# Inverting a head's diagonal 16-row blocks: substitution in blocks of 4 rows and doubling, in place of fifteen steps

## The chip, the cores and the metric

The kernel runs on one core of one Trainium2 chip. The metric is the device time of one launch in microseconds, the median of several runs. The engines are named as the profile names them: PE (TensorE, matmuls), PEld (its weight loads), DVE (VectorE), ACT (ScalarE), POOL (GpSimd) and SP (SyncE, which issues most of the DMAs). Each engine works through a queue of its own in order, and engines wait for each other by semaphores.

## The reference

One layer of a streaming encoder for 16 meta tokens, 512 tokens of a prompt and 8 x 16 tokens of samples (656 together): layer norm, one input projection, then two groups of heads side by side (a gated delta rule in 8 heads of 128, and a complex diagonal state space of 64 groups), an output projection, layer norm, a gated feed-forward of 2048 by 5632, layer norm. What matters here is the gated delta rule, which is computed block by block; for each block a unit lower triangular system is solved:

```python
a_mat = jnp.where(strict, jnp.einsum('bhnid,bhnjd->bhnij', kb, k) * decay, 0.0)
rhs = jnp.concatenate([v * beta[..., None], kb * jnp.exp(gcum)[..., None]], axis=-1)
sol = lax.linalg.triangular_solve(a_mat, rhs, left_side=True, lower=True, unit_diagonal=True)
w_val, k_cd = sol[..., :dv], sol[..., dv:]
...
def step(s, xs):
    w = w_val_c - jnp.einsum('bhcd,bhde->bhce', k_cd_c, s)
    o = jnp.einsum('bhcd,bhde->bhce', q_dec_c, s) + jnp.einsum('bhij,bhje->bhie', qk_c, w)
    s = s * g_tot_c[..., None, None] + jnp.einsum('bhcd,bhce->bhde', k_dec_c, w)
```

## The kernel before

The stages follow one another: layer norm and the state space's tables, the projections of the state space group, the heads' stage (`heads_phase`, from about 400 to 1000 us), the output projection, and the feed-forward, which is most of the time. In the heads' stage PE's queue is filled with the "fill": the projections q, k, v of heads 2 to 7 and z of all heads (`project`: for each of 16 row tiles and each half of the tokens three matmuls, L505, L506 and L507, on the two parts `whi` and `wlo` of a weight). The weights come in as float32 `raw`; ACT makes `whi` (L160), and in this stage POOL makes `wlo` (L161). The fill's results go through a convolution on DVE (L646, three times L649, L656, L657) and ACT (L634 to L636, L653, L654).

Among the fill's steps `drive` sets side jobs, generators which go on one step at a time; PERIOD = 47 steps of the fill lie between one head and the next. For each head these are

- `delta_prep`: the products k k^T and q k^T of the head's 6 units (tokens in groups of 112, 112, 112, 96, 96 and, for the samples, 128), then `inv16`, then the factors of the units (L839 and others);
- `delta_double`: the inverses grow from 16 rows to a whole unit. POOL makes `gm` (L860), PE multiplies it with `tt` (L863), ACT copies the product (`pp`, L864), PE multiplies again (L868), DVE subtracts it from `rt` (L870); then twice transposes (L393), copies of `tt` on ACT (L877), a product with `gt` (L885, copied by ACT in L886) and one with `rt` (L893);
- `delta_scan`: unit after unit through the state. PE multiplies the state `st` with k and q (L935, L936); DVE makes `rhs` (L938); PE solves with `rt` (L943); ACT scales to `x` (L945); PE makes the output's part (L948) and the state's part (L971); DVE adds the output into `vc` (L953) and updates `st` (L976), for which the next unit's L935 waits. The last unit, that of the samples, has its own path: L923 to L930 on PE, DVE and ACT, then `xm`, x spread over four masks (L958, DVE), and PE's L963 on it; POOL scales the samples' states `sb` (L964) and DVE adds to them (L967).

The scan of one head runs beside the preparation of the next ones. A tile scheduler sets the order of each engine's queue from these jobs, by its own estimates of the time at which an instruction can begin.

`inv16` inverts the 41 diagonal blocks of 16 rows of a head's units. Three DMAs bring `gt` to memory (L752), three fetch the blocks so that each block lies on a partition of its own (`blk`, 41 partitions x 16 x 16, L754). `t0` is set to the identity. Then for each column i from 1 to 15 a multiply of a column of `blk` (step of 16 elements) with the i x i corner of `t0` into `pr` (L760, i x i products) and a reduce of these along their rows (L762); every step needs the one before. A transposed copy (L765) makes the second half of `ti`, and six DMAs to memory (L768) and six back (L771) put both into `tt` and `rt`. The generator yields four times within the fifteen steps. In gelu, which runs in the same stage for the state space group, L1315 is a multiply of 128 x 640 elements, and L1318 one that writes with a step of four elements.

## Time and profile before

| | us |
| --- | --- |
| median of the runs (lowest, highest) | 3027.91 (3024.25, 3028.52) |
| the profiled execution: span | 3024.3 |
| PE busy | 2846.3 (94%) |
| PEld busy | 2721.0 (90%) |
| DVE busy | 2312.0 (76%) |
| ACT busy | 1171.5 (39%) |
| POOL busy | 595.9 (20%) |

The span is that of one execution on the profiler; there is nothing around it that a run's time would add. The chain of work that ended last, followed back from the end, has 53% of the span on PE, 13% on DVE, 3% on DMA and 1% each on ACT and POOL; 1% of the span in this chain is DVE's L760. The heads' stage is 600 us of the 3024.3. In the rows further down the first number is a start in microseconds from the start of the span and the second the duration, both in microseconds; what stands in brackets is the idle time of the engine in front of that row, and what ended it. In the table by stretches the column PEclk is the granted clock of PE as a share of 2.4 GHz (0.5 is 1.2 GHz).

### The profile page before, as it was taken

Reading aid. Unit: us, or ns where it says so; the run is one execution under the profiler, and the core shown is the slowest. Engines: PE = TensorE matmul, PEld = TensorE weight load, DVE = VectorE, ACT = ScalarE, POOL = GpSimd, SP = SyncE. Lnnn points to the kernel's source line nnn. Section 1 sums busy time; section 2 is a strip of 40 time slices with the busy share of each in tenths; the row PEclk is TensorE's granted clock in tenths of the full one; section 3 lists DMA queues with packets and bytes.
Section 4 is the critical chain, followed back from the end, with each engine's and each line's share of the span. In section 5 each row is a group of like instructions: output and inputs, shape, how many; then the busy total and the mean of one; then the engine's idle time right before and its main releaser. Section 6 shows DMA issues by size and latency. Waiting matters only on the chain.

```text
span 3024.3 us, 47836 instructions
## 1 busy us (share of the span) xinstructions
PE 2846.3 (94%) x18707; PEld 2721.0 (90%) x18707; DVE 2312.0 (76%) x4077; ACT 1171.5 (39%) x2127; POOL 595.9 (20%) x551
## 2 busy tenths in 40 slices
PE   5989899999999999979999999999999999999996
PEld 4989888888888978779999999999999999999995
DVE  8899867666665663697777777777777879888998
ACT  4445334333343522553333333333333443332334
POOL 4244423222222040240000000000000023321214
PEclk9999999899899999989999999999999999999998
DMA  4333333333344753543333333333343534433533
GB/s 152 84 103 98 96 105 84 80 82 86 90 134 141 244 167 103 170 121 118 101 115 99 115 103 113 113 113 112 105 119 99 168 115 145 131 115 115 174 120 125
DMA packets 460770, 360.67 MB, mean 119 GB/s; under 512 B 49364, under 2 KB 422276, under 8 KB 456432
## 3 DMA queue, kind: packets, MB, share of 16 engines
q1 hardware_dynamic: 458744, 354.50, 39.3%
q8 instruction: 147, 2.41, 0.3%
q10 hardware_dynamic: 1800, 3.11, 0.3%
q14 instruction: 79, 0.65, 0.1%
HBM read 295.55 MB, written 62.01 MB: 118 GB/s over the span
## 4 chain that ended last, share of the span: by engine, by line
PE 53%; DVE 13%; issue 4%; DMA 3%; ACT 1%; POOL 1%; SPq 0%; DVEq 0%; ACTq 0%; POOLq 0%
PE pb_m L1393 16%; PE pb_m L1392 16%; PE pb_m L1391 16%; DVE wlo L161 3%; DVE acf L1804 2%; DVE raw L193 2%; DMA rq<-in_ffn_w_down 1%; PE pj L505 1%; PE pj L506 1%; ACT whi L160 1%; PE pj L507 1%; POOL wlo L161 1%; DVE acc L1487 1%; DVE hp L1778 1%; DVE pr L760 1%
## 5 line engine op out<-in xcount | busy, mean ns | idle before, releaser
L160 ACT ACTIVATE whi<-raw 128x1024 fp32r<-128x1024 f32 x408 | 431.6, 1058 | 768.0 <-PE pb_m L1392 259.8
L161 DVE TENSOR_TENSOR wlo<-raw,whi 128x1024 fp32r<-128x1024 f32 x330 | 426.4, 1292 | 221.8 <-ACT whi L160 221.4
L505 PE MATMUL pj<-hh,whi 128*128 128x328 f32 (+1 forms) x1248 | 429.4, 344 | 1.9 <-DVE zs L1006 1.2
L506 PE MATMUL pj<-hl,whi 128*128 128x328 f32 (+1 forms) x1248 | 404.4, 324 | 0.0
L507 PE MATMUL pj<-hh,wlo 128*128 128x328 f32 (+1 forms) x1248 | 403.0, 323 | 0.0
L1393 PE MATMUL pb_m<-hp,wlo 128*128 128x320 f32 x1120 | 348.6, 311 | 21.9 <-DVE wlo L161 18.9
L1391 PE MATMUL pb_m<-hp,whi 128*128 128x320 f32 x1120 | 347.4, 310 | 2.2 <-ACT whi L160 2.2
L1392 PE MATMUL pb_m<-hp,whi 128*128 128x320 f32 x1120 | 346.9, 310 | 0.0
L160 ACT ACTIVATE whi<-rq 128x1024 fp32r<-128x1024 f32 x190 | 200.6, 1058 | 324.1 <-PE pb_m L1392 309.2
L161 POOL TENSOR_TENSOR wlo<-raw,whi 128x1024 fp32r<-128x1024 f32 x78 | 197.4, 2531 | 580.9 <-ACT whi L160 487.4
L1778 POOL TENSOR_TENSOR hp<-lq,hp 128x960 fp32r<-128x960 f32 (+1 forms) x16 | 47.5, 2976 | 1106.8 <-ACT hp L1777 1106.8
L505 PEld LDWEIGHTS pj<-hh,whi 128*128 128x128 f32 x1248 | 243.7, 195 | 12.4 <-issue 8.2
L506 PEld LDWEIGHTS pj<-hl,whi 128*128 128x128 f32 x1248 | 244.3, 196 | 2.1 <-issue 1.5
L507 PEld LDWEIGHTS pj<-hh,wlo 128*128 128x128 f32 x1248 | 243.7, 195 | 2.1 <-issue 1.5
L1393 PEld LDWEIGHTS pb_m<-hp,wlo 128*128 128x128 f32 x1120 | 211.7, 189 | 25.6 <-DVE wlo L161 21.7
L193 DVE TENSOR_TENSOR raw<-rq 128x1024 f32<-128x1024 f32 x128 | 163.4, 1276 | 86.9 <-DMA rq<-in_ffn_w_up 34.2
L161 DVE TENSOR_TENSOR wlo<-rq,whi 128x1024 fp32r<-128x1024 f32 x176 | 223.4, 1270 | 4.3 <-ACT whi L160 2.9
L1391 PEld LDWEIGHTS pb_m<-hp,whi 128*128 128x128 f32 x1120 | 211.8, 189 | 3.3 <-ACT whi L160 3.3
L1392 PEld LDWEIGHTS pb_m<-hp,whi 128*128 128x128 f32 x1120 | 211.6, 189 | 0.0
L1708 DVE TENSOR_TENSOR s<-pb_m,s 128x320 f32<-128x320 f32 x308 | 149.2, 485 | 71.9 <-PE pb_m L1393 69.3
L1804 DVE TENSOR_TENSOR acf<-acf,pb_m 128x320 f32<-128x320 f32 x368 | 163.4, 477 | 22.3 <-PE pb_m L1393 20.8
L1391 PE MATMUL pb_m<-T1h,whi 128*128 128x320 f32 x352 | 110.3, 313 | 2.6 <-ACT T1h L1544 2.6
(561 smaller groups left out, 7631.7 us busy)
## 6 DMA issues: line engine op xcount, KB each, us to landing
rq<-in_ffn_w_gate SPq DMA_DIRECT2D x88, 512.0 KB
rq<-in_ffn_w_up SPq DMA_DIRECT2D x88, 512.0 KB
raw<-in_w_in SPq DMA_DIRECT2D x80, 512.0 KB
rq<-in_ffn_w_down SPq DMA_DIRECT2D x80, 512.0 KB
raw<-in_w_out SPq DMA_DIRECT2D x48, 512.0 KB
scr_h<-hq SPq DMA_DIRECT2D x20, 1120.0 KB
lq<-scr_h SPq DMA_DIRECT2D x16, 640.0 KB
raw<-in_ffn_w_down SPq DMA_DIRECT2D x16, 512.0 KB
```

The costliest lines, as they stand in the source:

```text
L160: nc.scalar.activation(hi, val, AF.Copy)
L161: next(self.lows).tensor_sub(lo, val, hi.bitcast(F32))
L193: self.nc.vector.tensor_tensor(o, x, y, op=op)
L505: nc.tensor.matmul(o, whi[:, k], self.h_hi[u][:, k, s], start=(kk == 0), stop=False)
L506: nc.tensor.matmul(o, whi[:, k], self.h_lo[u][:, k, s], start=False, stop=False)
L507: self.last = nc.tensor.matmul(o, wlo[:, k], self.h_hi[u][:, k, s], start=False, stop=(kk == KT - 1))
L1391: mm(out, sh, mh, start=first, stop=False)
L1392: mm(out, sh, ml, start=False, stop=False)
L1393: self.last = mm(out, sl, mh, start=False, stop=last)
L1708: v.tensor_tensor(t, x, y, op=ALU.add)
L1778: (v if (j + g) % 2 else nc.gpsimd).tensor_sub(x[:, 1], t, x[:, 0].bitcast(F32))
L1804: v.tensor_tensor(x, x, ps, op=ALU.subtract if o[0] == "-" else ALU.add)
```

## The change

In place of fifteen steps over columns the block of 16 rows is inverted in three stages. First N is negated in place (L762). Then the four diagonal blocks of 4 rows are inverted at once, by substitution: a copy of 4 elements, and for columns 2 and 3 a multiply (L767, 16 and 36 products) and a reduce (L768). `blk`, `ti` and `pr` are wider (272 and 576 elements), so that the four blocks, which lie 68 elements apart, can be written as one access pattern. Then two doublings, from 4 to 8 and from 8 to 16 rows: each makes the block above the diagonal as T11 N12 T22, in two products. A product is a multiply (L782; for s = 4 twice 64 elements, for s = 8 once 512, patterns of four dimensions with a step of 16 elements in one operand) and reduces (L790 to the middle part of `pr`, L788 into `t0`). The copy and the DMAs behind it are as they were. The generator still yields four times: behind the substitution, behind both products for 4, and behind the first product for 8.

DVE has 20 instructions for a head where it had 33 (two memsets, a copy and thirty others before). Other lines of the diff take comments out, which moves line numbers behind `inv16` by 28: L935, L953, L976 are now L963, L981, L1004; L864, L870, L877 are L892, L898, L905; L958 and L963 (`xm` and its matmul) are L986 and L991.

```diff
-        blk = dl.tile([nb, 16, 16], F32, name="blk", tag="blk", bufs=1)
-        ti = dl.tile([nb, 2, 16, 16], F32, name="ti", tag="ti", bufs=1)
-        pr = dl.tile([nb, 225], F32, name="pr", tag="pr", bufs=1)
+        bk = dl.tile([nb, 272], F32, name="blk", tag="blk", bufs=1)
+        tk = dl.tile([nb, 2, 272], F32, name="ti", tag="ti", bufs=1)
+        pr = dl.tile([nb, 576], F32, name="pr", tag="pr", bufs=1)
+        whole = lambda x: x[:, :256].rearrange("b (c i) -> b c i", i=16)
+        fours = lambda x: x.rearrange("b (n x) -> b n x", x=68)[:, :, :64].rearrange("b n (c i) -> b n c i", i=16)[:, :, :, :4]
+        blk, t0, t1 = whole(bk), whole(tk[:, 0]), whole(tk[:, 1])
...
-        t0 = ti[:, 0]
-        v.memset(t0, 0.0)
-        v.memset(t0.rearrange("b c i -> b (c i)")[:, ::17], 1.0)
-        for i in range(1, 16):
-            p = pr[:, : i * i].rearrange("b (c j) -> b c j", j=i)
-            v.scalar_tensor_tensor(p, blk[:, :i, i][:, None, :].to_broadcast([nb, i, i]), -1.0, t0[:, :i, :i],
-                                   op0=ALU.mult, op1=ALU.mult)
-            v.tensor_reduce(t0[:, :i, i], p, axis=mybir.AxisListType.X, op=ALU.add)
-            if i in (4, 8, 11, 13):
-                yield
-        v.tensor_copy(ti[:, 1].rearrange("b i c -> b c i"), t0)
+        v.memset(tk[:, 0], 0.0)
+        v.memset(tk[:, 0, 0:256:17], 1.0)
+
+        v.tensor_scalar(bk[:, :256], bk[:, :256], -1.0, None, op0=ALU.mult)
+        b4, t4 = fours(bk), fours(tk[:, 0])
+        v.tensor_copy(t4[:, :, 0, 1], b4[:, :, 0, 1])
+        for i in (2, 3):
+            p = pr[:, : 4 * i * i].rearrange("b (n c j) -> b n c j", n=4, j=i)
+            v.tensor_tensor(p, b4[:, :, :i, i][:, :, None, :].to_broadcast([nb, 4, i, i]), t4[:, :, :i, :i], op=ALU.mult)
+            v.tensor_reduce(t4[:, :, :i, i], p, axis=mybir.AxisListType.X, op=ALU.add)
+        yield
+
+        for s in (4, 8):
+            n = 8 // s
+            mid = pr[:, 512 : 512 + n * s * s]
+            for right in range(2):
+                for k in range(n):
+                    lo, hi = slice(2 * s * k, 2 * s * k + s), slice(2 * s * k + s, 2 * s * k + 2 * s)
+                    p = pr[:, k * s**3 : (k + 1) * s**3].rearrange("b (r c k) -> b r c k", c=s, k=s)
+                    if right:
+                        x, y = mid[:, k * s * s : (k + 1) * s * s].rearrange("b (r c) -> b r c", c=s), t0[:, hi, hi]
+                    else:
+                        x, y = t0[:, lo, lo], blk[:, lo, hi]
+                    v.tensor_tensor(p, x[:, :, None, :].to_broadcast([nb, s, s, s]),
+                                    y.rearrange("b k c -> b c k")[:, None].to_broadcast([nb, s, s, s]), op=ALU.mult)
+                if right:
+                    for k in range(n):
+                        lo, hi = slice(2 * s * k, 2 * s * k + s), slice(2 * s * k + s, 2 * s * k + 2 * s)
+                        p = pr[:, k * s**3 : (k + 1) * s**3].rearrange("b (r c k) -> b r c k", c=s, k=s)
+                        v.tensor_reduce(t0[:, lo, hi], p, axis=mybir.AxisListType.X, op=ALU.add)
+                else:
+                    v.tensor_reduce(mid, pr[:, : n * s**3].rearrange("b (x k) -> b x k", k=s), axis=mybir.AxisListType.X, op=ALU.add)
+                if s == 4 or not right:
+                    yield
+        v.tensor_copy(t1.rearrange("b i c -> b c i"), t0)
         for c in range(2):
             for g in range(3):
-                nc.sync.dma_start(self.diag(sr[c], g), ti[rows[g], c])
+                nc.sync.dma_start(self.diag(sr[c], g), (t0, t1)[c][rows[g]])
```

The scheduler gives other orders between about 410 and 950 us; ahead of that and behind it the queues are the same. Three places follow. The first is DVE's queue within `inv16` of head 1, at about 469 us before: L953 and L976 belong to the scan of head 0. Before:

```order
L760 SCALAR_TENSOR_TENSOR pr<-blk,ti 41x49
L953 TENSOR_TENSOR vc<-o_5610,ps_seq 96x128
L762 TENSOR_REDUCE ti<-pr 41x7
L976 SCALAR_TENSOR_TENSOR st<-st,ee,ps_seq 128x128
L760 SCALAR_TENSOR_TENSOR pr<-blk,ti 41x64
```
After:

```order
L782 TENSOR_TENSOR pr<-pr,ti 41x64 x2
L788 TENSOR_REDUCE ti<-pr 41x4x4 x2
L782 TENSOR_TENSOR pr<-ti,blk 41x512
L790 TENSOR_REDUCE pr<-pr 41x64
L981 TENSOR_TENSOR vc<-o_5584,ps_seq 96x128
L782 TENSOR_TENSOR pr<-pr,ti 41x512
L1004 SCALAR_TENSOR_TENSOR st<-st,ee,ps_seq 128x128
L788 TENSOR_REDUCE ti<-pr 41x8x8
```
L953 and L976 (now L981 and L1004) stood between two small pairs; now one stands between the two wide multiplies and the other behind the second.

The second is DVE's queue in the samples' part of head 4's scan, at about 773 us before. Before:

```order
L930 SCALAR_TENSOR_TENSOR o_9003<-ps_seq,own,o_9003 128x128
L646 TENSOR_SCALAR yc<-xp,cwc 128x680
L649 SCALAR_TENSOR_TENSOR yc<-xp,cwc,yc 128x680 x2
L953 TENSOR_TENSOR vc<-o_9003,ps_seq 128x128
L958 TENSOR_TENSOR xm<-x,consts 128x512
L649 SCALAR_TENSOR_TENSOR yc<-xp,cwc,yc 128x680
L967 TENSOR_TENSOR sb<-sb,ps_seq 128x512
```
After:

```order
L958 SCALAR_TENSOR_TENSOR o_8925<-ps_seq,own,o_8925 128x128
L646 TENSOR_SCALAR yc<-xp,cwc 128x680
L649 SCALAR_TENSOR_TENSOR yc<-xp,cwc,yc 128x680 x2
L898 TENSOR_TENSOR rt<-rt,ps_inv 96x5x3x16
L986 TENSOR_TENSOR xm<-x,consts 128x512
L981 TENSOR_TENSOR vc<-o_8925,ps_seq 128x128
L649 SCALAR_TENSOR_TENSOR yc<-xp,cwc,yc 128x680
L995 TENSOR_TENSOR sb<-sb,ps_seq 128x512
```
`xm` still follows two of the three L649, but the doubling's subtraction (L870, now L898), which stood further back, is now in front of it.

The third is ACT's queue at the same place. Before:

```order
L929 ACTIVATE o_9003<-ps_seq,own 128x128
L945 ACTIVATE x<-ps_seq,fc 128x128
L160 ACTIVATE whi<-raw 128x1024
L954 ACTIVATE jk_9075,ms<-vc 128x128
L653 ACTIVATE kq<-yc 128x528
L864 ACTIVATE pp_4510<-ps_inv 96x15x16
L654 ACTIVATE kq<-yc 128x128
L877 ACTIVATE tt<-ps_inv 32x5x32
L877 ACTIVATE tt<-ps_inv 32x3x32
```
After:

```order
L957 ACTIVATE o_8925<-ps_seq,own 128x128
L973 ACTIVATE x<-ps_seq,fc 128x128
L892 ACTIVATE pp_4510<-ps_inv 96x15x16
L905 ACTIVATE tt<-ps_inv 32x5x32
L905 ACTIVATE tt<-ps_inv 32x3x32
L982 ACTIVATE jk_8997,ms<-vc 128x128
L160 ACTIVATE whi<-raw 128x1024
L914 ACTIVATE pp<-ps_inv 32x5x32
```
L160, which makes the next `whi` and which POOL's L161 waits for, stood behind `x` (L945); it now stands behind the doubling's copies L892 and L905 and L982.

## Rows read from the trace of the kernel before

**Rows 1.** The page, busy time of each engine (share of the span), instructions:

```profile
PE 2846.3 (94%) x18707; PEld 2721.0 (90%) x18707; DVE 2312.0 (76%) x4077; ACT 1171.5 (39%) x2127; POOL 595.9 (20%) x551
```

**Rows 2.** Table by stretch: length; busy PE, PEld, DVE, ACT, POOL; PEclk, DMA share, GB/s:

```profile
400.00:1100.00 700.00, 658.45 (x4421) 596.85 (x4420) 474.58 (x1241) 281.08 (x843) 203.18 (x148) 0.94 0.43 121
630.00:646.00 16.00, 14.35 (x69) 9.65 (x68) 8.94 (x30) 2.41 (x9) 0.85 (x2) 0.57 0.30 83
776.00:796.00 20.00, 17.50 (x88) 13.07 (x87) 9.37 (x29) 3.53 (x11) 0.99 (x1) 0.57 0.22 57
919.00:926.00 7.00, 4.97 (x34) 4.38 (x34) 3.56 (x11) 1.45 (x6) 1.90 (x1) 0.76 0.37 74
```

**Rows 3.** Groups of DVE, 400 to 1000 us: count | busy us, mean ns | idle before:

```profile
L760 DVE SCALAR_TENSOR_TENSOR pr<-blk,ti 41x1 f32<-41x1 f32 (+14 forms) x120 | 62.9, 524 | 3.9 <-DMA blk<-scr_g 0.9
...
L762 DVE TENSOR_REDUCE ti<-pr 41x1 f32<-41x1 f32 (+14 forms) x120 | 27.7, 231 | 3.1
```

**Rows 4.** Timeline of DVE in inv16, heads 1 and 7:

```profile
466.36 0.14 DVE L760 SCALAR_TENSOR_TENSOR pr<-blk,ti 41x1 f32<-41x1 f32 x1
...
469.33 0.33 DVE L976 SCALAR_TENSOR_TENSOR st<-st,ee,ps_seq 128x128 f32<-128x128 f32 x1
...
471.36 2.04 DVE L760 SCALAR_TENSOR_TENSOR pr<-blk,ti 41x121 f32<-41x121 f32 x1
...
476.40 0.55 DVE L760 SCALAR_TENSOR_TENSOR pr<-blk,ti 41x225 f32<-41x225 f32 x1
476.99 0.38 DVE L762 TENSOR_REDUCE ti<-pr 41x15 f32<-41x225 f32 x1
...
905.09 0.14 DVE L760 SCALAR_TENSOR_TENSOR pr<-blk,ti 41x1 f32<-41x1 f32 x1
```

**Rows 5.** Timeline of POOL in head 1 and in scans 2 and 4:

```profile
470.76 2.49 POOL L161 TENSOR_TENSOR wlo<-raw,whi 128x1024 fp32r<-128x1024 f32 x1 [7.05 <-ACT whi L160]
...
625.78 2.39 POOL L161 TENSOR_TENSOR wlo<-raw,whi 128x1024 fp32r<-128x1024 f32 x1 [4.41 <-ACT whi L160]
...
773.95 3.05 POOL L161 TENSOR_TENSOR wlo<-raw,whi 128x1024 fp32r<-128x1024 f32 x1 [1.64 <-ACT whi L160]
```

**Rows 6.** Single lines on DVE: duration in ns, min/median/max:

```profile
L958 DVE TENSOR_TENSOR xm<-x,consts x8: 677/678/685, 487.8 to 988.3; 128x512 f32<-128x512 f32 x8
...
L1318 DVE SCALAR_TENSOR_TENSOR ge<-gt__9621,yf x1: 1284/1284/1284, 837.8 to 837.8; 128x640 f32<-128x640 f32 x1
...
L649 DVE SCALAR_TENSOR_TENSOR yc<-xp,cwc,yc x72: 900/919/2911, 146.9 to 810.6; 128x680 f32<-128x680 f32 x72
```

**Rows 7.** Waits of PE from 400 to 1000 us: total us, times, longest:

```profile
PE ps_seq L935 <- DVE st L976: 8.8, 8, 3.0
PE ps_seq L963 <- DVE xm L958: 6.4, 3, 2.5
PE ps_seq L943 <- DVE rhs L938: 3.3, 3, 1.5
...
PE ps_seq L923 <- DVE vc L953: 3.0, 3, 2.0
```

**Rows 8.** Timeline of PE where its waits end:

```profile
470.84 0.38 PE L935 MATMUL ps_seq<-st,kq 128*96 128x128 f32 x2
...
632.02 1.22 PE L963 MATMUL ps_seq<-xm,kd 64*128 64x512 f32 x1 [1.65 <-DVE xm L958]
...
778.57 1.97 PE L963 MATMUL ps_seq<-xm,kd 64*128 64x512 f32 x2 [2.50 <-DVE xm L958]
...
911.43 0.46 PE L935 MATMUL ps_seq<-st,kq 128*96 128x128 f32 x2 [1.65 <-DVE st L976]
...
921.04 1.07 PE L923 MATMUL ps_seq<-sb,kq 128*32 128x256 f32 x16 [2.03 <-DVE vc L953]
```

**Rows 9.** Timeline of DVE ahead of xm in scans 2 and 4:

```profile
625.98 5.38 DVE L649 SCALAR_TENSOR_TENSOR yc<-xp,cwc,yc 128x680 f32<-128x680 f32 x2
...
773.85 3.87 DVE L649 SCALAR_TENSOR_TENSOR yc<-xp,cwc,yc 128x680 f32<-128x680 f32 x2
```

## The prediction

> **What bounds the kernel now.** I read the engines' busy times first: PE is busy for 94% of the span, DVE for 76%, POOL for 20% [rows 1]. So a shorter DVE chain is worth only what PE now waits for it. The change touches the heads' stage alone, and the table by stretches shows there, from 400 to 1100 us, 658.45 of 700 us of PE and a mean clock of 0.94 [rows 2]: some 42 us of idle and, as 0.06 of 700, another 42 us lost to half clock. In the same table three short stretches stand at 0.57, 0.57 and 0.76 [rows 2], each from the end of one wait of PE [rows 8]: the granted clock falls from 2.4 to 1.2 GHz behind such waits, and stays there for longer than the wait was. The third view is the list of PE's waits in this stage [rows 7]: DVE's state update L976 (8.8 us), DVE's `xm` L958 (6.4), `rhs` L938 (3.3), `vc` L953 (3.0). All four are short operations that stand in DVE's queue among the instructions of `inv16` or behind them. The last view is the timeline of DVE in head 1 [rows 4]: fifteen pairs of multiply and reduce, one waiting for the other, from 466.36 to 477.37, 11.0 us, and a copy behind them; four other instructions, which the scan of the head before needs, stand between them.
>
> **The change: DVE's own time.** By the groups of DVE instructions, L760 took 62.9 us in 120 instructions and L762 27.7 [rows 3]. One clean multiply is 0.14 us for one product and 0.55 for 225 [rows 4], so 0.14 + 1.8 ns a product; 1240 products in 15 instructions are 2.1 + 2.23 = 4.33 us a head, 34.7 in eight. The other 28.2 us are stalls: the 121-product multiply took 2.04 us, and POOL's L161 ran from 470.76 to 473.25 beside it [rows 4, 5]. A reduce is 0.38 for 225 [rows 4], so 0.14 + 1.07 ns a product, 27.7 / 8 = 3.46 a head; I see no stalled reduce.
> After: multiplies on 16, 36, four times 64 and twice 512 products, 8 x 0.14 + 1332 x 1.8 ns = 3.52; reduces on 16, 36, 128, 64, 64, 512, 512, 7 x 0.14 + 1332 x 1.07 ns = 2.41; the negation of 256 elements between the smallest multiply and that of 225 products, 0.14 and 0.55 [rows 4], taken at 0.25 because it reads one operand as the reduce does; the copy of four 0.14. Together 6.32 against 7.79, and 13 instructions fewer, each with about 0.04 us to the next (476.95 to 476.99) [rows 4], 0.52: 2.0 us a head, 16 in all. The memsets and the transposed copy stay.
> The wide multiply has no row. A 512-element product with both operands read along rows took 0.68 (L958); one of 640 elements with a step of four elements on its output took 1.28, 2.0 ns an element (L1318) [rows 6]. So one of 512 costs 0.68 to 1.16; I take 0.14 + 0.92 = 1.06, from the line through L760's rows, because its column operand has the same step of 16 elements. Both together move a head by -0.8 to +0.2.
> [...]
> Stalls: 28.2 / 8 = 3.5 us a head, so a chain is 11.0 - 1.7 (head 1's own stall) + 3.5 = 12.8 us on average; one that is two to four us shorter and spends less time in two-operand multiplies (3.5 for 4.3) should keep about 2.6. That is 0.9 a head, 7 in all. DVE's busy time falls by some 23 us (16 without the stalls' part, 30 with the low price of the wide multiply). None of it is time of the span yet: PE has its fill, the projections' matmuls L505 to L507, for nearly all of it.
>
> **What of it reaches PE.** The chain ends about 2 us earlier where no stall falls out and 4 or 5 where one of some 2 us does. The doubling behind it (L863, L868, now L891, L896) moves 2 to 7 triples of the fill forward in PE's queue, and with it everything on ACT and DVE.
> Gains. (a) Waits in which PE stood for something of DVE that was held up by a stalled multiply: L943's 3.3, of which I count two thirds, 2.2, and L923's 3.0, whose `vc` stood behind the end of the chain (the longest, 2.03, at 921.04) [rows 7, 8]: 5.2 us together; and the fall of the clock behind the last, 7 x 0.24 = 1.7 [rows 2]. (b) Scan 4: PE waited 2.50 us for `xm` at 778.57 [rows 8], because two L649 in front of it took 3.87 us in place of 1.84 (0.92 each in the median), stalled by POOL's L161 from 773.95 [rows 5, 6, 9]. That L161 waits for ACT's L160; in the new order L160 stands behind the doubling's copies L892 and L905, so the POOL operation starts behind the two L649. PE has `xm` when it comes for it: 2.50 + (1 - 0.57) x 20 = 11.1 us [rows 2]. (c) Scan 2 likewise: 1.65 at 632.02, two L649 of 5.38 us under L161 from 625.78 [rows 5, 8, 9]; L160 moves behind L905, and PE's order has the doubling's first product and transposes well ahead of `xm`. 1.65 + 0.43 x 16 = 8.5 us [rows 2]. In scans 1 and 3 PE's waits of the same kind keep their neighbours, and I leave them as they are.
> Costs. (d) The new wait. Fifteen small pairs let a scan's L953 and L976 in after at most half a microsecond; the new order puts them behind the wide products. In head 1 L976 ended at 469.66 and PE came for it at 470.84 [rows 4, 8]. Now it (L1004) stands behind the second wide multiply: 6.32 - 0.69 for the last reduce, + 0.3 for L981 + 16 x 0.04 = 6.6 into the chain, end at 466.36 + 6.6 + 0.33 = 473.3, so 2.4 us late; and POOL's L161 from 470.76 [rows 5] then lies on a wide multiply, so up to 2 more: 4.3. In head 7 it stands behind both wide multiplies and two operations of gelu (0.83 and 1.28, as L1318 [rows 6]): 9.0 us into the chain, which began at 905.09, against 6.3 (L935 waited for it until 911.43) [rows 4, 8]: 2.7. In heads 2 to 6 it stands behind the second wide multiply (2), the first (3 to 5) or the copy (6), by the same sum 0.3 to 1.7 us later each, 4.9 together; there is no slack to take it, since L935 waited for L976 8 times [rows 7]. Sum 11.9 us, between 7 (no stall meets a wide multiply, and half of the small ones are hidden) and 16. Queued behind L1004 on DVE are the rest of the chain and the next `rhs`; who waits for it is PE's L935, and in PE's queue the whole fill stands behind that. (e) Waits of two us and more bring the clock down: the one of 2.03 us cost 1.7 [rows 2, 8], the one of 1.65 before 911.43 none that I see. I count three new falls, 5.1 us (none to five).
> DMAs: the number and the order of the transfers of a head are the same (3, 3, 6, 6), nothing passes SP's queue, and `tt` comes earlier with the end of the chain.
> Sum: -5.2 - 1.7 - 11.1 - 8.5 + 11.9 + 5.1 = -9.5 us. The profiled execution's span of 3024.3 us is that of the fastest of the three runs, 3.6 below their median; so 3024.3 - 9.5 + 3.6 = about **3018 us**.
>
> **Rivals.** (B) No change: one of the two `xm` waits stays or a new one of its size comes. `xm` in scan 2 is only about a microsecond earlier by the queue (a POOL product L964 that now comes first would hold L656 instead, and L898 is now in front of `xm`). For it: the new order puts L898 ahead of `xm` in four scans, and L898 waits for PE. Against: PE's own `xm` matmuls stand further back. With one of (b), (c) lost the sum is -1 to +2: 3027 to 3030 us. (C) Slower: the wide multiplies are where stalls now land. Of the 120 multiplies of 0.14 to 0.55 us some 13 were held up (28.2 us by 2.1 each); one of 1.06, with L1004 behind it, is met oftener, and in each such head PE waits 2 us more and loses 1.7 to the clock. If it is so in six heads and not in two, (d) and (e) grow by 4 x 3.7 = 15, and (c) is lost for the same reason: -9.5 + 15 + 8.5 = +14, 3042 us. It decides from the fourth head on in which L1004 ends behind a stalled wide multiply. For it speaks 28.2 us of stalls in this very line; against, that the chain is shorter. (D) The change doesn't do what it says: the wide products, of four dimensions, run at 2.1 us each with nothing beside them, twice my price; then a head's chain is no shorter than before (-2.0 + 2.1), the doubling is no earlier, neither `xm` wait goes (+19.6), and L1004 is another 1 to 2 us later in six heads: about +19, 3047 us.
>
> **How the numbers follow.** Forecast 0.50, B 0.25, C 0.19, D 0.06. About 0.2%, 6 us, is what a measurement of this kernel can tell from no change. The forecast's case holds sums from -20 ((d) at 7, no new falls) to -3, so a tenth of it counts as no change, and a part of B goes beyond 6 us on either side: faster 0.51, same 0.25, slower 0.24. The range goes from the forecast's best sum, 3024.3 - 20 + 3.6 = 3008, less 2 for the low price of the wide multiplies, to most of C: 3006 to 3037 us.
>
> **What would show it.** In the changed kernel's profile: 120 and 120 instructions replaced by 64 multiplies and 56 reduces, wide multiplies at 1.0 to 1.1 us where no POOL operation lies beside them; DVE's busy time 16 to 30 us less between 400 and 1100 us; no wait of PE for `xm` in scans 2 and 4, and the clock at 1.0 around 640 and 785 us; L935's waits for L1004 at some 20 us where they were 8.8, the longest in heads 1 and 7. I am wrong on the sign if `xm` still comes late (look whether the L649 before it are stalled, or L898 waits for PE), or if L935's waits exceed 30 us; wrong on the mechanism if the chains are not two to five us shorter.

## The result: 1.1% faster, three times what was forecast

The changed kernel takes 2997.96 us in the median (2986.92 to 3001.62) where the kernel before, on the same chip, takes 3028.18: a ratio of 0.9892, interval 0.9871 to 0.9912, or 30 us. The forecast was 10 us, and its range reached down to 3006 us. The direction and most of the mechanism were right; the size was not. The page of the changed kernel, span and busy times (the time of this execution is 2995.59 us, 1.8 above its span):

```profile
span 2993.8 us, 47732 instructions
...
PE 2819.4 (94%) x18707; PEld 2704.2 (90%) x18707; DVE 2283.6 (76%) x3973; ACT 1171.5 (39%) x2127; POOL 594.2 (20%) x551
```

DVE lost 28.4 us and PE 26.9 us of busy time against [rows 1], though PE does the same 18707 matmuls. Where the 30.5 us between the two spans went can be followed by a clock that both traces have, the copies that ACT makes out of `pj`, which end a projection of the fill and come in the same order in both. The start of the same copy, before and after:

| copy of `pj`, behind | before, us | after, us | difference |
| --- | --- | --- | --- |
| head 0's preparation | 406.3 | 404.1 | -2.2 |
| (head 2's chain) | 544.4 | 544.9 | +0.5 |
| scan 1's samples | 601.9 | 596.4 | -5.5 |
| scan 2's samples | 649.4 | 636.3 | -13.1 |
| scan 3's samples | 723.7 | 704.3 | -19.3 |
| scan 4's samples | 806.2 | 778.2 | -28.1 |
| all of the heads' stage | 1002.8 | 974.7 | -28.2 |

The first 2.2 us are ahead of anything that the change moves, and 2.3 more lie behind 1003 us, where the queues are the same; both are of the size by which two executions of one program differ (in the profiles of the kernels below the first copy comes 1.3 to 6.3 us earlier than before). The 26 us between come in four steps, one for each of scans 1 to 4, of 6, 8, 6 and 9 us by this table; ahead of them, in head 0's part, the changed kernel gives 2.7 us back.

Between the first and the last of these copies PE has 3875 matmuls in both kernels. Before, then after (length; busy PE, PEld, DVE, ACT, POOL; PEclk, DMA share, GB/s):

```profile
406.30:1002.80 596.50, 558.78 (x3875) 507.69 (x3874) 392.81 (x1105) 229.48 (x730) 165.71 (x133) 0.93 0.40 107
404.10:974.70 570.60, 534.20 (x3875) 493.48 (x3874) 364.33 (x1005) 230.40 (x731) 164.06 (x133) 0.97 0.41 111
```

PE stood idle for 37.7 us of the first and 36.4 of the second. So of the 25.9 us the waits in sum gave 1.3. By the trace's record of the granted clock PE was at half clock for 78.6 us here before and for 34.0 after (the record has shares of 1 and 0.5 alone; in the kernel before, the fill's matmuls of 320 columns start every 267 ns at 0.5, which is 1.2 columns a ns, and every 147 ns at 1). Half of that difference is 22.3 us, an estimate as if all of PE's work took twice as long there; by the fill's 147 for 267 ns it is 20: the gain is nearly all clock. The table by stretch (length; busy PE, PEld, DVE, ACT, POOL; PEclk, DMA share, GB/s), after:

```profile
400.00:1100.00 700.00, 659.88 (x4516) 603.11 (x4515) 455.41 (x1145) 284.87 (x845) 200.28 (x145) 0.97 0.45 127
550.00:566.00 16.00, 13.99 (x103) 11.22 (x102) 12.29 (x25) 4.26 (x13) 5.76 (x3) 0.79 0.06 20
616.00:632.00 16.00, 15.45 (x138) 12.95 (x137) 12.93 (x29) 5.70 (x17) 5.08 (x5) 1.00 0.41 109
688.00:704.00 16.00, 15.17 (x130) 13.31 (x129) 12.52 (x35) 6.07 (x17) 3.05 (x3) 1.00 0.20 54
750.00:770.00 20.00, 19.64 (x165) 16.39 (x164) 13.75 (x36) 7.82 (x22) 4.64 (x4) 1.00 0.58 125
```

The last four are the samples' parts of scans 1 to 4. Two of the same parts before stand in [rows 2] at 0.57; those of scans 1 and 3 read, before:

```profile
550.00:580.00 30.00, 27.79 (x163) 22.46 (x162) 16.36 (x36) 8.43 (x28) 7.62 (x4) 0.72 0.42 89
702.00:721.00 19.00, 16.62 (x90) 11.88 (x89) 9.80 (x30) 3.31 (x11) 2.15 (x2) 0.64 0.27 72
```

By the same record PE stood at half clock for 17.1, 13.7, 13.7 and 17.1 us in these four parts before, and for 6.8, 0, 0 and 0 after. PE's waits from 400 to 1000 us (total, times, longest) are now others than in [rows 7], though not fewer; `xm` (L986) is no longer among them:

```profile
PE ps_seq L963 <- DVE st L1004: 15.9, 10, 3.7
PE ps_seq L393 <- DVE vc L1016: 4.7, 3, 2.2
PE ps_seq L971 <- DVE rhs L966: 3.8, 6, 1.0
PE ps_inv L891 <- DMA tt<-scr_r: 2.8, 1, 2.8
PE ps_inv L393 <- DVE rt L898: 2.6, 2, 2.0
```

DVE's timeline in head 1, which answers to [rows 4]:

```profile
466.44 1.04 DVE L782 TENSOR_TENSOR pr<-ti,blk 41x512 f32<-41x512 f32 x1
467.52 0.68 DVE L790 TENSOR_REDUCE pr<-pr 41x64 f32<-41x512 f32 x1
468.13 0.27 DVE L981 TENSOR_TENSOR vc<-o,ps_seq 96x128 f32<-96x128 f32 x1
468.32 1.02 DVE L782 TENSOR_TENSOR pr<-pr,ti 41x512 f32<-41x512 f32 x1
469.26 0.34 DVE L1004 SCALAR_TENSOR_TENSOR st<-st,ee,ps_seq 128x128 f32<-128x128 f32 x1
469.52 0.67 DVE L788 TENSOR_REDUCE ti<-pr 41x64 f32<-41x512 f32 x1
470.23 2.25 DVE L793 COPY ti<-ti 41x256 f32<-41x256 f32 x1
```

The wide multiplies are 1.04 and 1.02 us, as priced (1.06); L1004 stands behind both. The stall of this head now falls on the copy, since POOL is at work beside it:

```profile
469.86 2.38 POOL L161 TENSOR_TENSOR wlo<-raw,whi 128x1024 fp32r<-128x1024 f32 x1 [8.82 <-ACT whi L160]
```

### The profile page after: what moved, and what is told of

Read it like the earlier page. It is cut to its first block, busy times and chain, and to the rows that moved or that the text cites. A ratio compares the mean times of both kernels' runs of the same rounds, so it can differ in the third digit from the quotient of the medians.

```text
span 2993.8 us, 47732 instructions
## 1 busy us (share of the span) xinstructions
PE 2819.4 (94%) x18707; PEld 2704.2 (90%) x18707; DVE 2283.6 (76%) x3973; ACT 1171.5 (39%) x2127; POOL 594.2 (20%) x551
## 3 DMA queue, kind: packets, MB, share of 16 engines
q1 hardware_dynamic: 458744, 354.50, 39.9%
## 4 chain that ended last, share of the span: by engine, by line
PE 66%; DVE 22%; issue 5%; DMA 4%; ACT 2%; POOL 1%; SPq 0%; DVEq 0%; ACTq 0%; POOLq 0%
PE pb_m L1419 17%; PE pb_m L1421 17%; PE pb_m L1420 17%; PE pj L505 3%; PE pj L507 3%; PE pj L506 3%; DVE wlo L161 3%; DVE raw L193 2%; DVE acf L1832 1%; DVE yc L649 1%; ACT whi L160 1%; DMA u<-scr_u 1%; POOL wlo L161 1%; DMA raw<-in_w_out 1%; DVE pr L782 1%
## 5 line engine op out<-in xcount | busy, mean ns | idle before, releaser
L160 ACT ACTIVATE whi<-raw 128x1024 fp32r<-128x1024 f32 x408 | 431.6, 1058 | 766.2 <-PE pb_m L1420 260.4
L161 DVE TENSOR_TENSOR wlo<-raw,whi 128x1024 fp32r<-128x1024 f32 x330 | 427.9, 1297 | 222.8 <-ACT whi L160 222.5
L160 ACT ACTIVATE whi<-rq 128x1024 fp32r<-128x1024 f32 x190 | 200.5, 1058 | 325.3 <-PE pb_m L1420 311.5
L161 POOL TENSOR_TENSOR wlo<-raw,whi 128x1024 fp32r<-128x1024 f32 x78 | 194.8, 2498 | 566.2 <-ACT whi L160 465.0
L161 DVE TENSOR_TENSOR wlo<-rq,whi 128x1024 fp32r<-128x1024 f32 x176 | 222.7, 1266 | 4.1 <-ACT whi L160 2.7
```

Source lines behind the costliest of these rows:

```text
L160: nc.scalar.activation(hi, val, AF.Copy)
L161: next(self.lows).tensor_sub(lo, val, hi.bitcast(F32))
```

## The experiments

Two theories to begin with. **O**: the gain is the place of the doubling on PE. A shorter chain lets the scheduler put its products and transposes ahead of the samples' part of the scan, and the waits and the half clock that came of their meeting go. **D**: the gain is DVE's 28 us of time. All ratios are against the kernel before on the same chip. "Stretches" are PE's stretches at half clock, from one profiled execution of each kernel.

**b_scan2**: the kernel before, and the place moved by other means.

```diff
-            jobs.append((self.delta_scan(h), 26, at + 54, at + 2 * PERIOD + 14))
+            jobs.append((self.delta_scan(h), 26, at + 56, at + 2 * PERIOD + 16))
```

> The kernel before, fifteen steps untouched, with the scan's jobs two steps of the fill later (54 and 14 become 56 and 16), so that in scans 0 to 3 PE's queue has the doubling's products and transposes ahead of the samples' xm, as in the changed kernel; in scans 4 and 5 it has not. Theory O (the gain is the place of the doubling against the samples' part of the scan, and the clock behind it): the long half-clock stretches at 557, 632 and 707 us (17.1, 13.7, 13.7 us) go or shrink to 7 or less, the one at 779 stays; about 18 us faster, 3010 us (3003 to 3018). Theory D (the gain is DVE's 28 us of time less): nothing was taken from DVE, 3028 us (3022 to 3034).

Measured: 0.9931 (0.9914 to 0.9948), 3006 us. DVE's time is nearly that of before (2304 us). The stretches at scans 1 to 4 are 0, 0, 10.2 and 10.2 us. By the table of stretches, scans 1 to 4 (the 0.94 of the first two is a stretch of 3.4 us each, behind a later wait for something else):

```profile
545.00:575.00 30.00, 27.44 (x217) 23.77 (x216) 20.39 (x50) 12.71 (x41) 8.00 (x6) 0.94 0.37 98
620.00:650.00 30.00, 27.83 (x212) 24.90 (x212) 19.32 (x57) 12.29 (x44) 6.22 (x7) 0.94 0.41 103
690.00:712.00 22.00, 20.00 (x139) 16.78 (x138) 13.90 (x34) 6.62 (x20) 7.59 (x4) 0.77 0.29 74
764.00:780.00 16.00, 13.71 (x78) 9.88 (x77) 9.70 (x29) 3.00 (x11) 1.42 (x1) 0.68 0.19 50
```

Scan 3's stretch was expected at 7 us or less. Two thirds of the gain come with nothing taken from DVE. D falls as the whole cause. The edit moves the scan against the convolution as well as against the doubling, so by itself it does not tell which of the two meetings counts.

**a_scanm2**: the changed kernel with the place moved back (52 and 12 in the same line).

> The changed kernel with the scan's jobs two steps of the fill earlier (52 and 12), so that PE's queue has the doubling's first products within two fill steps of xm again, as before the change, with the short inv16 kept. Theory O: waits for xm or rt with half-clock stretches of 10 us and more come back in three or four of the scans 0 to 4; 3018 us (3010 to 3030). Theory D: DVE's time is as in the changed kernel, 2998 us (2990 to 3004).

Measured: 1.0018 (1.0002 to 1.0034), 3030 us: all of the gain is gone with the short chain kept. Stretches of 10.2, 13.7 and 17.1 us are back in scans 0, 1 and 4. It is not a pure test: the earlier scan also meets the next head's preparation, and PE waited 14.7 us for `qk` (L837) there.

**a_pad_chain** and **a_pad_behind**: the same four wide multiplies a head added, 33 us of DVE by their clean price, in the chain or behind it. Here the scan stays where it is.

```diff
-                    v.tensor_tensor(p, x[:, :, None, :].to_broadcast([nb, s, s, s]), ...)
+                    for _ in range(5 if s == 8 and right else 1):            # a_pad_chain
+                        v.tensor_tensor(p, x[:, :, None, :].to_broadcast([nb, s, s, s]), ...)
```

> The changed kernel with its second wide multiply done five times over (same operands, same result): four times 1.04 us more in each head's chain, 4.2 us a head, 33 us of DVE in all. The chain is as long as before the change and PE's queue has the doubling where it was before. Theory O: the four long half-clock stretches come back and L1004 waits for two wide multiplies more; 3036 us (3026 to 3048). Theory D: 33 us of DVE time more than the changed kernel, 3030 us (3024 to 3036). The two theories agree here; it is to be read beside a_pad_behind.

> The changed kernel with the same four wide multiplies a head, but behind the chain's last copy and its DMAs, where nothing waits for their result: the same 33 us of DVE time, the same order on PE as in the changed kernel. Theory O: 3001 us (2994 to 3010), a little for what stands behind them on DVE. Theory D: as a_pad_chain, 3030 us (3024 to 3036).

Measured: 1.0044 (1.0029 to 1.0059) in the chain, 0.9932 (0.9915 to 0.9948) behind it. The table by stretch from 400 to 1000 us, of a_pad_chain:

```profile
400.00:1000.00 600.00, 548.44 (x3806) 500.24 (x3805) 408.73 (x1008) 222.76 (x715) 174.57 (x135) 0.93 0.37 99
```

and of a_pad_behind:

```profile
400.00:1000.00 600.00, 556.53 (x3971) 515.77 (x3971) 416.23 (x1071) 239.00 (x757) 169.09 (x134) 0.95 0.41 111
```

DVE is as busy in the second as in the first (416 and 409 us; over the whole span the first has 12 us more, 2339 and 2327), and 33 us lie between the two kernels. It is not the state update either: PE's waits for it are 16.5 us in the first and 15.8 in the second. What counts is when the chain ends, since that sets where the doubling stands. a_pad_behind was expected at 3001 and took 3007: DVE time is not quite free.

**b_noxm**: one wait taken away, the place of the doubling kept. L963 reads zeros, so the kernel leaves the samples' own tokens out of their new states.

```diff
-                    mm(pb[q], kd[r, u], xm[r].rearrange("p b e -> p (b e)"), start=True, stop=True)
+                    mm(pb[q], kd[r, u], self.xz[r], start=True, stop=True)
```

> The kernel before with the matmul L963 reading a tile of zeros that is set once, in place of xm, which DVE still computes (so the samples' new states leave the update by their own tokens out): the chain, DVE's time and the place of the doubling are as before the change, and only the wait for xm is gone; L963 moves a few places forward on PE. Theory W (the long half-clock stretches come from the wait itself): the waits of 2.2, 1.7 and 2.5 us and the stretches at 557, 632 and 779 us go, the one at 707, behind a wait for pp, stays; 3028 - 6.4 - 24 = about 2998 us (2994 to 3008). Theory M (they come from the small matmuls of the doubling and of the samples standing together, whether PE waits or not): the stretches stay at 13 us and more, 3022 us (3016 to 3028).

Measured: 0.9959 (0.9943 to 0.9974), 3016 us, between the theories. In scans 1 and 2 PE now waits at the next place, for `rt` from the doubling's subtraction (here L872), which stands behind the same held-up pair of L649. In scan 1:

```profile
554.08 5.26 DVE L649 SCALAR_TENSOR_TENSOR yc<-xp,cwc,yc 128x680 f32<-128x680 f32 x2
...
560.70 0.39 DVE L872 TENSOR_TENSOR rt<-rt,ps_inv 96x240 f32<-96x240 f32 x1
```

PE, at the end of that wait:

```profile
561.14 0.62 PE L393 MATMUL ps_inv<-ident,rt 96*96 96x96 f32 x5 [1.79 <-DVE rt L872]
```

The stretches of scans 1 to 4 are 10.2, 10.2, 13.7 and 0: only scan 4's went, where the longest wait left is 1.09 us. Neither W nor M as put: the small matmuls alone do not bring the clock down in scan 4, and in scans 1 and 2 the wait passes on.

**b_jk**: the same question for scan 3, where PE had waited for ACT's `pp`. ACT's rows before:

```profile
704.62 0.31 ACT L954 ACTIVATE jk<-vc 128x128 f32<-128x128 f32 x1 [4.15 <-DVE vc L953]
704.84 0.19 ACT L954 ACTIVATION_READ_ACCUMULATOR jk<-vc 128x1 f32 x1
704.93 0.35 ACT L864 ACTIVATE pp<-ps_inv 96x240 f32<-96x240 f32 x1
```

The copy of `pp` stood behind a square (L954) that waited 4.15 us for DVE. The edit puts the square of the samples' unit one job step later:

```diff
-            a.activation(tmp("jk2", 1)[:n], o, AF.Square, accum_out=ms[:n, u : u + 1])
+            if u != SU:
+                a.activation(tmp("jk2", 1)[:n], o, AF.Square, accum_out=ms[:n, u : u + 1])
...
                 nc.sync.dma_start(io["o_delta_s"][0, :, h].rearrange("b d e -> d b e"), sb)
+                yield
+                a.activation(tmp("jk2", 1)[:n], o, AF.Square, accum_out=ms[:n, u : u + 1])
```

> The kernel before with one thing moved: for the samples' unit ACT takes the square of the output (L954) one job step later, so that the copy of pp (L864) no longer stands behind it on ACT. PE's order is that of before. If scan 3's wait for pp (2.38 us, and 13.7 us at half clock) has this cause of its own, both go and nothing takes their place: 3028 - 2.4 - 6.9 = 3019 us (3014 to 3022). If any single wait taken away is followed by the next (xm, which ended at 705.97 in the kernel before, then rt), PE waits 1 to 2 us for xm in scan 3 in its place, the stretch stays at 10 us or more, and the time is 3026 us (3022 to 3031).

Measured: 1.0003 (0.9986 to 1.0019). The wait for `pp` is gone, and the next one is there, with a stretch of 10.2 us:

```profile
709.62 1.12 PE L964 MATMUL ps_seq<-xm,kd 64*128 64x512 f32 x2 [1.84 <-DVE xm L959]
```

**b_half161** and **a_half161**: POOL's operation that holds DVE, in two halves, in both kernels.

```diff
-            next(self.lows).tensor_sub(lo, val, hi.bitcast(F32))
+            e = next(self.lows)
+            for c in ((slice(0, w),) if e is not nc.gpsimd else (slice(0, w // 2), slice(w // 2, w))):
+                e.tensor_sub(lo[:, c], val[:, c], hi[:, c].bitcast(F32))
```

> The kernel before with POOL's making of wlo in the heads' stage in two operations of 512 columns in place of one of 1024; the order on PE, ACT and DVE is that of the kernel before. If the late xm, pp and rt in scans 1 to 4 come from DVE's L649 being held for the whole of a POOL operation (3.87 and 5.3 us for two in place of 1.84), DVE gets in between the halves: pairs of L649 at 2.5 to 3.5 us, xm's waits 1 us or less in two of the scans at least, one or two of the four long half-clock stretches gone, 3014 us (3004 to 3022). If the stall is not what makes them late (the order alone is): the stretches stay, 3027 us (3022 to 3033).

Measured: 0.9945 (0.9929 to 0.9962), 3014 us, as expected, but not for the reason expected. The pair of L649 (here L651) is 3.55 us where it was 5.26; POOL's next operation (L966, 2.52 us from 552.57) then holds `xm` itself, 2.38 us where L958 took 0.68 [rows 6]:

```profile
549.78 3.55 DVE L651 SCALAR_TENSOR_TENSOR yc<-xp,cwc,yc 128x680 f32<-128x680 f32 x2
553.25 2.38 DVE L960 TENSOR_TENSOR xm<-x,consts 128x512 f32<-128x512 f32 x1
```

PE's waits for `xm` stay (6.5 us, 3 times) and the stretches are 13.7, 10.2, 13.7 and 17.1. Of the profiled execution's 12.6 us, 6.3 lie ahead of the first copy of the table above, 5.6 of them ahead of the first halved operation. The other 6.2 are spread over the stage and are not clock: PE's idle time there is 31.5 us for 37.7, its time at half clock 81.9 for 78.6. By its ratio the kernel wins some 17 us; the rest was not placed.

> The changed kernel with the same halves. Its stalls on DVE (blk's negation 2.5 us in head 6, gelu's multiply 2.8 in head 7, two L649 5.25 in scan 1) are cut by half if DVE gets in between: L1004's waits 12 us in place of 15.9, 2992 us (2984 to 3000). If POOL's halves run back to back with DVE still held out: 2998 (2990 to 3004).

Measured: 0.9846 (0.9831 to 0.9862), 2984 us: the fastest kernel that computes everything, and faster than the changed kernel by more than both intervals. The expected cause was missed here too: L1004's waits are 16.0 us as before the halves. One thing that went is scan 1's last stretch. In the changed kernel:

```profile
551.41 5.25 DVE L649 SCALAR_TENSOR_TENSOR yc<-xp,cwc,yc 128x680 f32<-128x680 f32 x2
...
556.58 0.39 DVE L898 TENSOR_TENSOR rt<-rt,ps_inv 96x240 f32<-96x240 f32 x1
```

and with halves:

```profile
547.48 3.55 DVE L651 SCALAR_TENSOR_TENSOR yc<-xp,cwc,yc 128x680 f32<-128x680 f32 x2
550.95 0.39 DVE L900 TENSOR_TENSOR rt<-rt,ps_inv 96x240 f32<-96x240 f32 x1
```

`rt` comes 1.7 us earlier behind the pair, PE's wait for it falls from 2.01 to 0.30 us, and the clock stays up. So in scan 1 the shorter stall ended a wait where the doubling stands ahead of `xm`, and handed it on where it does not. That is 3.4 us of the 7.1 by which the stage is shorter than the changed kernel's; another 3.3 are idle time of PE (33.1 us for 36.4). By the ratios halving is worth about as much in either place, 0.0055 before the change and 0.0046 after it.

**b_scan2h**: b_scan2 and b_half161 together, the fifteen steps untouched.

> The kernel before, fifteen steps untouched, with the scan's jobs two steps later (as in b_scan2, which gave 0.9931) and POOL's wlo in two halves (as in b_half161, 0.9945). If place and stalls are all there is, the new inverse is not needed for most of the gain: 2993 us (2986 to 3002). If the two act on the same waits, no better than b_scan2: 3006 us (3002 to 3012).

Measured: 0.9905 (0.9877 to 0.9934), 2995 us: what the change gives, without it.

**a_scan1** and **a_scan2**: more distance (55 and 15, 56 and 16).

> The changed kernel with the scan's jobs one step of the fill later (55 and 15): the doubling's products and transposes stand ahead of the samples' part in scans 0 to 4 with six or more of the fill between, and partly in scan 5. If the place is what counts, the remaining stretches in scans 0 and 1 (3.4 and 6.8 us) go and the time is 2993 us (2985 to 3000); if more distance buys nothing, 2998.

> The changed kernel with the scan's jobs two steps later (56 and 16): the doubling, with its first transposes and products, is wholly ahead of the samples' part in all scans but the last. Place: 2992 us (2984 to 3000). No more than the changed kernel's gain: 2998. Every scan ends two steps, 3 us, later, of which the last is outside the fill and may cost up to 3 us.

Measured: 0.9921 (0.9891 to 0.9952) and 0.9941 (0.9920 to 0.9962): both missed, no better than the changed kernel or worse. The samples' part then meets another stretch of the convolution, POOL holds `xm` itself in some scans (2.38 us for 0.68), and PE waits for it again, with two steps more 8.6 us in four scans. Of the four places tried with the short chain the changed kernel's is the best.

**b_short** and **a_half**: the cost of L1004's place, from both sides. b_short leaves out the last four columns of each block's inverse.

```diff
-        for i in range(1, 16):
+        for i in range(1, 12):                                # b_short
...
+                    for r in (slice(0, 4), slice(4, 8)):      # a_half, for s = 8: multiply, reduce, multiply, reduce
```

> The kernel before with only the first eleven of its fifteen steps (the last four columns of each block's inverse are left as the identity's), yields at 4, 7, 9 and 10: a chain some 4 us shorter, of small pairs alone, with no wide multiply. PE's queue has the doubling ahead of the samples' part in scans 0 to 4, as in the changed kernel. If the place of the doubling gives the gain and the wide multiplies take some of it back through L976 (15.9 us of waits where there were 8.8, with half-clock stretches behind three of them): L976's waits at 8 to 10 us and 2988 us (2980 to 2996). If the wide multiplies cost nothing beside it: 2998 us (2994 to 3004). If the gain needs the new instructions themselves: 3024 us or more.

> The changed kernel with each wide product as two halves of 256 products, each multiply followed by its reduce: 0.9 us a head more of DVE, and the scheduler puts L981 and L1004 (here L991 and L1014) behind all four in heads 1 to 4 and 7, 1 to 3 us later than in the changed kernel. A dose of the cost of the state update behind the wide products: its waits 15.9 us to 24 to 30, with two or three more half-clock stretches of 3.4 us; the place of the doubling is as in the changed kernel in scans 0 to 4. 3010 us (3002 to 3018) if each microsecond of that wait is a microsecond of the span and more; 2998 if it is hidden.

Measured: 0.9854 (0.9833 to 0.9875) and 0.9919 (0.9902 to 0.9937). PE's waits for the state update, in b_short:

```profile
PE ps_seq L935 <- DVE st L976: 8.1, 9, 3.0
```

and in a_half:

```profile
PE ps_seq L973 <- DVE st L1014: 20.5, 10, 3.9
```

8.1, 15.9 (changed kernel) and 20.5 us of this wait go with 0.9854, 0.9892 and 0.9919: 20 us of time over 12 us of wait. That would fit a price of some 10 us for the wide multiplies, through the state update, but does not show it: b_short also has less work on DVE and a chain that ends earlier, and a_half has 13.7 us at half clock in scan 4, behind a wait for `rt`, where the changed kernel has none.

**a_pool**: the wide multiplies on POOL.

```diff
-                    v.tensor_tensor(p, x[:, :, None, :].to_broadcast([nb, s, s, s]),
+                    (v if s == 4 else nc.gpsimd).tensor_tensor(p, x[:, :, None, :].to_broadcast([nb, s, s, s]),
```

> The changed kernel with the two wide multiplies of each head on POOL, so that DVE's queue has no instruction of 1.04 us in front of L981 and L1004. If these two wide multiplies are what holds the state update (15.9 us of waits where the short-chain kernel has 8.1): L1004's waits at 8 to 11 us. But a POOL multiply with a step of 16 elements may take 1.2 to 2.5 us, waits behind L161 (2.4 us) in POOL's queue, and DVE's own two-operand work is held beside it. Taken together: 2996 us (2984 to 3012); over 3005 the chain has become longer than the fifteen steps' and the doubling is late on PE.

Measured: 0.9895 (0.9880 to 0.9909), no gain over the changed kernel. The wide multiplies took 1.60 and 1.61 us in the mean on POOL, for L161's 2.46. L1004's waits are down as expected, another wait takes their place, and the time stays; what L1004's place costs in time is open:

```profile
PE ps_seq L971 <- DVE rhs L966: 12.1, 9, 2.6
PE ps_seq L963 <- DVE st L1004: 8.8, 8, 3.0
```

The kernels side by side. "Ahead" is in how many of scans 0 to 4 PE's queue has the doubling's first transposes ahead of `xm`'s first matmul. The next two columns give the stretches at half clock in the samples' parts of scans 1 to 4 (those behind later waits for something else are left out) and in head 0. "Half" and "idle" are all of PE's time at half clock and all of its idle time between the first and the last copy of the table above. All but the ratio are from the profiled executions, in us.

| kernel | ahead | scans 1, 2, 3, 4 | head 0 | half | idle | ratio |
| --- | --- | --- | --- | --- | --- | --- |
| before | 0 | 17.1, 13.7, 13.7, 17.1 | 6.8 | 78.6 | 37.7 | 1 |
| b_jk | 0 | 17.1, 17.1, 10.2, 20.5 | 23.9 | 102.4 | 37.4 | 1.0003 |
| a_pad_chain | 0 | 13.7, 13.7, 13.7, 17.1 | 6.8 | 81.9 | 52.1 | 1.0044 |
| a_scanm2 | 0 | 13.7, 0, 0, 17.1 | 23.9 | 102.4 | 47.0 | 1.0018 |
| b_noxm | 0 | 10.2, 10.2, 13.7, 0 | 20.5 | 64.9 | 35.8 | 0.9959 |
| b_half161 | 0 | 13.7, 10.2, 13.7, 17.1 | 23.9 | 81.9 | 31.5 | 0.9945 |
| b_scan2 | 4 | 0, 0, 10.2, 10.2 | 6.8 | 37.5 | 39.9 | 0.9931 |
| b_scan2h | 4 | 0, 0, 0, 13.7 | 23.9 | 47.8 | 33.0 | 0.9905 |
| a_scan1 | 5 | 6.8, 0, 0, 0 | 23.9 | 47.8 | 39.2 | 0.9921 |
| a_scan2 | 5 | 0, 6.8, 6.8, 6.8 | 23.9 | 61.4 | 42.2 | 0.9941 |
| a_pad_behind | 5 | 10.2, 0, 0, 0 | 23.9 | 54.6 | 43.5 | 0.9932 |
| a_half | 5 | 6.8, 0, 0, 13.7 | 13.7 | 61.4 | 41.9 | 0.9919 |
| a_pool | 5 | 3.4, 0, 10.2, 0 | 23.9 | 44.4 | 40.8 | 0.9895 |
| after | 5 | 6.8, 0, 0, 0 | 10.2 | 34.0 | 36.4 | 0.9892 |
| a_half161 | 5 | 0, 0, 0, 0 | 13.7 | 27.3 | 33.1 | 0.9846 |
| b_short | 5 | 0, 0, 3.4, 0 | 10.2 | 23.9 | 31.4 | 0.9854 |

All kernels with the doubling ahead in four or five scans have 24 to 61 us at half clock, those without 65 to 102. The place is not all: a_scan2 has it in five scans and wins less than the changed kernel, and a_half has 13.7 us at half clock in scan 4 with it. In which way the place brings the clock down, by waits alone or by what PE does behind them, no run here separates.

## Why the prediction was right in kind and too small

**DVE's own time** came near, in part by luck: 23 us were expected (16 to 30) and 28.4 measured. The sum had 16 us for the work itself, which fell by 12 (4 of the 16 are gaps between instructions, which busy time does not hold), and 7 for the stalls, which fell by 16. The prices held: 1.04 for 1.06 us, the reduce of 512 at 0.68 for 0.69. The DVE groups, 400 to 1000 us (count | busy us, mean ns | idle before):

```profile
L782 DVE TENSOR_TENSOR pr<-pr,ti 41x64 f32<-41x64 f32 (+1 forms) x24 | 13.6, 591 | 0.3
L782 DVE TENSOR_TENSOR pr<-ti,blk 41x64 f32<-41x64 f32 (+1 forms) x24 | 12.3, 535 | 0.3
...
L762 DVE TENSOR_SCALAR blk<-blk 41x256 f32<-41x256 f32 x8 | 7.7, 957 | 1.5 <-DMA blk<-scr_g 1.5
...
L793 DVE COPY ti<-ti 41x256 f32<-41x256 f32 x8 | 6.8, 849 | 0.2
```

The stalls are 28.2 us before, 21 expected, some 12 after. With L767's 3.9 the multiplies take 29.8 us, 1.6 over the clean 28.2; the negation has 5.5 us of stall (7.7 less 8 x 0.28), the copy 3.8 (6.8 less 8 x 0.38), the copy of four 0.9. The wide multiply took 1.04 us, not the 0.68 of L958 [rows 6], which was the low price; that this price would take 2 us off the time, as the lower end of the forecast's range has it, no run shows.

**Gains (b) and (c)**, scans 4 and 2, were right in place, cause and size: 11.1 and 8.5 us expected, steps of 9 and 8 measured. The two L649 ahead of `xm` are no longer held, and POOL's L161 starts behind `xm` in both scans (at 625.84 and 760.25 us). DVE in scans 2 and 4:

```profile
623.33 1.88 DVE L649 SCALAR_TENSOR_TENSOR yc<-xp,cwc,yc 128x680 f32<-128x680 f32 x2
625.13 0.68 DVE L986 TENSOR_TENSOR xm<-x,consts 128x512 f32<-128x512 f32 x1
...
755.31 1.89 DVE L649 SCALAR_TENSOR_TENSOR yc<-xp,cwc,yc 128x680 f32<-128x680 f32 x2
```

**The step that failed** is the sentence on scans 1 and 3, "PE's waits of the same kind keep their neighbours, and I leave them as they are". They gave 6 us each, 12 of the 20 us by which the forecast was short. Parted into waits and clock, the forecast's terms are 2.6 us more of waits and 12.1 less of half clock; the runs showed 1.3 less of waits and 22.3 less of half clock, and 12.0 of these are the stretches of scans 1 and 3 (half of 17.1 + 13.7 - 6.8 us). In scan 3 the order already showed it: the third pair of order rows, at scan 4, has `pp`'s copy (L892) move ahead of the square (L982) on ACT, and the same happens in scan 3, whose wait was for `pp`. In scan 1 DVE's pair of L649 still takes 5.25 us and PE still waits 2.01 us, for `rt`; but the stretch behind it is 6.8 us and not 17.1. I had priced waits one by one, where they are one bundle: b_noxm and b_jk show that a single wait taken away is followed by the next, and b_scan2 that another place of the scan against the doubling takes most of the half clock away at once.

**Cost (d)** was right in mechanism and too high: 15.9 us of waits for L1004 where about 20 were expected, 7.1 more than before for my 11.9. In heads 1 and 7 L1004 stands where I put it. The wait in head 7 is 3.73 us, but in head 1 it is 0.92 where I had 4.3, since the stall fell on the copy behind it; the second longest, 3.36, is head 6's, whose negation POOL held. **Cost (e)**: outside head 0 and scans 1 to 4 there are five stretches of 3.4 us for three before, 3.4 us net, as expected (5.1 less 1.7). Between 400 and 1000 us of the two profiled executions all 13 waits of PE of 1.99 us or more were followed by half clock, as (e) has it for two us and more; of the 10 waits of 1.3 to 1.8 us two were, the 1.65 us for `xm` in scan 2 and 1.60 us for `qk` at 877.65, both before. The chains are 4.2 us shorter in the mean, 10.1 us for 14.3 from the first multiply or the negation to the end of the copy, as expected.

**Gain (a)** held by half: `vc` for the samples (L923's 3.0 us) is gone, `rhs` is 3.8 us where it was 3.3. That (a) was too high and (d) too high as well cancels in part, by chance.

Rival B's worry, that PE waits for L898, did come in scan 1 (2.01 us), and once more for 0.6 us. C and D did not happen. The remaining 4.5 us of the difference (2.2 ahead of the stage and 2.3 behind it) lie where the change moves nothing; I put them down to the two executions.

## What to carry to other kernels

Where short stretches of half clock follow waits, read them as a group: look which two pieces of work meet on the engines there, and price what moves one of them past the other, not each wait alone. PE's idle time hardly changed here; its clock did. Before writing new arithmetic to shorten a chain, try the two numbers that say when the neighbouring job runs: here moving a job by two steps and halving one POOL operation gave the same 1% with the old arithmetic. A wide instruction in place of many small ones made those wait here that used to slip in between (15.9 us of PE's waits for the state update, for 8.8); look for the short, waited-for operation in its engine's queue.

## What the runs showed of the hardware

Some DVE instructions took longer beside a POOL operation. Of the multiplies, the one of 121 products took 2.04 us beside POOL's L161 [rows 4, 5] and 0.36 in head 0, with no POOL operation beside it. In the changed kernel the negation of `blk` took 2.49 us in head 6 (POOL's L161 at 806.01 for 2.62) and the copy of `ti` 2.25 in head 1, where they take 0.28 and 0.38 alone; both read one tile, where the multiply reads two. No reduce was held: 0.68 us at most, also beside POOL's L161, and in the kernel before 14 reduces that lie wholly within one took 0.35 at most.

How long PE stayed at half clock behind a wait went, in these traces, with what it did next. Where it went on with the fill, the record shows 3.4 us in nearly all cases, even behind waits of 3.4 to 3.7 us (both of these in the changed kernel, at 812 and 885 us); where the doubling's and the samples' matmuls followed, mostly 7 to 24 us, behind waits that were mostly 1.3 to 4.2. In head 0, with the same work behind the same wait of 2.3 to 4.2 us, it was 6.8 to 23.9 us from one kernel to the next. Half of that spread is 8.5 us, an estimate of its price, which may be part of why the changed kernel's own runs spread over 15 us; it was not tried.
